# One streaming encoder layer on one core: order of the first loads, stored q weights, and who scales the FFN's sums

## The chip, the core and the metric

The kernel runs on one core of one Trainium2 chip. A core has five engines with a queue of instructions each: TensorE (PE, with PEld for the loads of its weights), VectorE (DVE), ScalarE (ACT), GpSimd (POOL) and SyncE (SP, which here only issues DMAs). Each engine runs its own queue in program order and waits on semaphores for the others. Sixteen DMA engines move the data between the main memory and the core. The metric is the device time of one execution in microseconds. The kernel before took 3031.0 us, the median of three runs (3030.57 to 3031.74).

## The reference

One layer of a streaming encoder over 2048 prompt tokens and 64 sample tokens, in float32, with 1024 channels:

```python
mod = silu(c) @ w_ada + b_ada                  # six vectors of 1024 a token kind
sh1, sc1, gt1, sh2, sc2, gt2 = split(mod, 6)
h = rms_norm(x, norm1_g) * (1 + sc1) + sh1
glu_a, glu_b, q, k, v, g_conv, g_attn = split(h @ w_in, ...)
u = glu_a * sigmoid(glu_b)
conv_out = silu(layer_norm(depthwise_conv(u, 31) + b_dw)) @ w_conv_out
o = attend(rms_norm(q), rms_norm(k), v, rel_bias)      # chunks of 64, a band of 9
merged = sigmoid(g_conv) * conv_out + sigmoid(g_attn) * (o @ w_attn_out)
x = x + gt1 * (merged @ w_o)
h2 = rms_norm(x, norm2_g) * (1 + sc2) + sh2
gate, up = split(h2 @ w_ffn_in)
x = x + gt2 * ((silu(gate) * up) @ w_ffn_out)
```

Beside both streams' x the last rows of the convolution's input and of k and v are given out.

## The kernel before

**Products.** Each float32 factor is split into a high and a low part, and one product is three matmuls (`mm3`). A weight comes as raw floats into a staging buffer (`wst`, `wup` or `wfo`, L370), ACT rounds it to `whi`, and DVE or POOL makes the rest, `wlo<-wst,whi`. The class `Weights` holds five such pairs; `split` (L445) chooses the engine. Weights that several blocks use (`KEPT`, among them the q, k and v columns, key `("qkv", part, k)`) are written to memory as two halves after their first split (L493), and later blocks read both halves.

**Phase 1** goes over blocks of 576, 512, 512 and 512 tokens: norm, q, k and v, the convolution's GLU, gates and attention. Its start (`first_block`, L882) is a piece by itself. The token rows `x_t` are asked for first (L1082, SP), then four 512 KB slabs of `w_ada` (`Slabs.fill`, L241, tile `wmod`, also SP); ACT's queue issues the small vectors (L764 to L769). From `silu(c)`, made of ACT's `th` and written to `cl`, PE makes the slabs' products `pa<-wmod,cl`; DVE copies them to `R`, a product with `sel` turns them, and DVE makes the columns `A` and `B`. The rows of x are scaled by their norm `r` (DVE `t`, POOL `r<-t,mhalf`), turned by PE (`pt<-ident,x_t`), and DVE makes `h<-pt,A,B`, split into `hh` and `hl`. The eight turns of k alternate with modulation's next slabs, and `taps` (L796) loads the convolution's small vectors by SP.

**Phase 2** goes over 576, 768 and 768 tokens (s = 0, 1, 2): merge, `wo`, residual and second norm, FFN. The FFN uses sums of blocks of weights in place of some products; these sums `ws` (two inputs of 128x512) are made by POOL once, at s = 0, and stored in `sum_d` (L417). `presum` (L437) makes the next ones as soon as their raw weights have landed. In `residual` (L1649) a row of tokens gets its mean square (DVE `t`), its `r` by POOL, and ACT scales it to `xn`, which PE turns. PE fills the time with products of the other rows (`wo` over k, of which the first four are shared by all rows of a chunk), and with the first FFN products, `early`.

**The end of a block.** The FFN's sums stand in `acc`, twelve pieces of 128x512 at s = 1 and 2. For these blocks `scale` (L2003) multiplies each piece by the gate row `gt` and then adds the residual input `x1`, both on DVE, one instruction at a time, as a lane of work between the other steps. Then `add_last` (L2029) multiplies the products `pd` of the last two rows of `w_ffn_out` by the gate in PSUM, adds them to `acc`, and sends the piece out (L2045). At s = 0 the gate and x1 are applied at the end by another path.

All arithmetic is issued by one helper (L102), so the profile's groups differ by tile names and shapes. The order of a queue is fixed when the program is built, by lanes of work and an estimate of each engine's load.

Of the kernel before, what the change touches and what calls it, by code (L numbers as in the profile page):

```python
# [229 lines left out]
class Slabs:  # L230


    def __init__(self, sync, pool, stream, keys, source, held):
        self.sync, self.pool, self.stream, self.keys, self.source, self.held = sync, pool, stream, keys, source, held
        self.ready, self.used, self.given, self.freed = [], 0, 0, 0

    def fill(self):
        while len(self.ready) < min(len(self.keys), self.freed + self.held):
            (src,), a, b = self.source(self.keys[len(self.ready)])
            w = self.pool.tile([P, a, b], F32, tag="wmod", name="wmod", bufs=self.held)  # L240
            self.sync.dma_start(w, src)  # L241
            self.ready.append(w)
# [18 lines left out]
class Weights:  # L261
# [5 lines left out]
    def __init__(self, engines, pool, dram, stream, keys, source, staging, held, kept):  # L267
        self.stream = stream
        self.sync, self.act, self.dve, self.gps = engines
        self.pool, self.dram, self.keys, self.source = pool, dram, keys, source  # L270
        self.staging, self.held = staging, held
        self.sum_pool, self.sum_d, self.sums, self.hold, self.landed = None, None, {}, 0, {}

        self.room, self.leaving = {"wst": 1, "wup": 0, "wfo": 0}, {"wst": 0, "wup": 0, "wfo": 0}
# [123 lines left out]
    def operand(self, f, op):  # L398
# [38 lines left out]
    def presum(self):  # L437

        i = len(self.ready)
        if i in self.first and all(self.landed.get(j, 1e18) <= self.stream.load["pe"] for j in self.need[i]):  # L440
            for f, op in self.keys[i][1:]:
                if op[0] == "s":
                    self.operand(f, op)

    def split(self):  # L445
# [17 lines left out]
        on_dve = key[0] in ("in", "qkv") or turn % 2  # L463
# [25 lines left out]
        def then():  # L489
            if key in self.again and key not in self.stored:  # L490
# [21 lines left out]
    def fill(self):  # L512

        while self.available() and len(self.ready) - self.freed < self.held:
            self.split()
# [88 lines left out]
def streaming_layer(ctx: ExitStack, tc: tile.TileContext, I, O):  # L604
# [155 lines left out]
    def setup():  # L760
# [4 lines left out]
        nc.scalar.dma_start(r0[8:16], by_row(I["c_sample"][0]))  # L765
        o = 0
        for name in ("norm1_g", "norm2_g", "b_dw", "conv_ln_g", "conv_ln_b", "b_ada"):
            a = by_row(I[name][0])
            nc.scalar.dma_start(r1[o : o + a.shape[0]], a)  # L769
            o += a.shape[0]  # L770
        pt = ps_g.tile([P, 512], F32, tag="gp", name="pt")
# [4 lines left out]
        act.activation(th, cc, AF.Tanh, scale=0.5)  # L776
        dve.scalar_tensor_tensor(th, th, 1.0, cc, ALU.add, ALU.mult)
        dve.tensor_scalar(cl[:, :, :2], th.rearrange("p (s k) -> p k s", s=2), 0.5, None, ALU.mult)
        dve.memset(cl[:, :, 2:], 0.0)
        dve.memset(sel, 0.0)  # L780
        dve.tensor_reduce(sel[:, :2], ident.rearrange("p (j s) -> p s j", j=4)[:, :2], AX.X, ALU.add)
# [14 lines left out]
        def taps():  # L796
            for i in range(2):
                for j, g in enumerate((I["q_norm_g"], I["k_norm_g"])):
                    nc.sync.dma_start(gqk[HD * i : HD * i + HD, j : j + 1], g.rearrange("o d -> d o"))
            nc.sync.dma_start(gk, I["k_norm_g"].to_broadcast([P, HD]))  # L800
            cc = wk.tile([HIST, CONV], F32, tag="pr", name="cc", bufs=8)
            nc.sync.dma_start(cc, I["cache_conv"][0, 0])
            r2 = wk.tile([TAPS, CONV], F32, tag="pr", name="r2", bufs=8)
            nc.sync.dma_start(r2, I["w_dw"][0])
# [8 lines left out]
        return vectors, taps  # L813
# [64 lines left out]
    def first_rows():  # L878
        places = ((wa, "x", 3), (wa, "x", 3), (wa, "x", 3), (wk, "kk", 1), (wk, "q2", 1))
        return [load_x(*tl, *place) for tl, place in zip(token_tiles(*PBLOCKS[0]), places)]  # L880

    def first_block(xs):  # L882

        tiles = token_tiles(*PBLOCKS[0])
        vectors, taps = setup()
        taps = taps()
        for x_t, (t, n) in zip(xs, tiles):
            r = square(x_t, n)
            dve.tensor_scalar(x_t[:n], x_t[:n], r, None, ALU.mult)

        def modulation(ct):
# [3 lines left out]
            for c6, c in enumerate(cs):  # L895
                mod_sums(pa[:, c], [("mod", c6, ct // 2, h, 0) for h in range(2)])
# [8 lines left out]
        def turn(k):  # L905
# [26 lines left out]
        for k in range(KT - 2):  # L932
            if k == 2:
                next(taps)
# [3 lines left out]
            for i in range(len(tiles)):  # L938
                if i == 2 and not k:
                    rest = modulation(k + 2)  # L940
                if i == (2 if k else 4) and k % 2 == 0:
# [138 lines left out]
    def load_x(t, n, pool, tag, bufs):  # L1080
        x_t = pool.tile([P, D], F32, tag=tag, name="x_t", bufs=bufs)
        nc.sync.dma_start(x_t[:n], rows(x_p, x_s, t, n))  # L1082
# [566 lines left out]
    def residual(pp, t, n, gt1, a, half, hs, free, last, i):  # L1649
# [24 lines left out]
        r = rsqrt_mean(wk, ssq[:n], n, 1, D, 4)  # L1674
        yield stream.when("pool")
# [63 lines left out]
    for s, (lo, hi) in enumerate(CBLOCKS):  # L1739
# [4 lines left out]
        for i, (c0, c1) in enumerate(chunks):  # L1744
# [40 lines left out]
            for k in range(4):  # L1785
                for i in range(len(grp)):
                    wo(i, k)
            for i, (t, n) in enumerate(grp):
                for k in range(4, KT):
# [213 lines left out]
        def scale():  # L2003
# [6 lines left out]
            for i, t, n, j in pieces():  # L2010
                dst = acc[i][:n, 512 * j : 512 * j + 512]
                dve.tensor_tensor(dst, dst, gt[j][:n], ALU.mult)
                yield stream.when("dve")
            yield lambda: "x1" in ends and stream.load["pe"] > ends["landed"]
            for k, (i, t, n, j) in enumerate(pieces()):
                dst = acc[i][:n, 512 * j : 512 * j + 512]
                dve.tensor_tensor(dst, dst, ends["x1"][k // 3][:n, k % 3], ALU.add)
                ends["merged"] = k
                yield stream.when("dve")
# [9 lines left out]
        def add_last(ws):  # L2029

            for k, (i, t, n, j) in enumerate(pieces()):
# [5 lines left out]
                while ends.get("merged", -1) < k:  # L2037
# [5 lines left out]
                stream.at(  # L2043
                    stream.when("dve") + OUT_LAG,
                    lambda t=t, n=n, f=f, dst=dst: nc.sync.dma_start(rows(y_p, y_s, t, n)[:, f], dst),  # L2045
                )
            for _ in ws:
                W.done()

# [87 lines left out]
        stream.flush()  # L2137

# [28 lines left out]
```

## Time and profile before

| what | value |
|---|---|
| median of three runs | 3031.0 us (3030.57 to 3031.74) |
| the profiled execution | 3030.89 us |
| its span | 3029.1 us |
| PE, DVE, ACT, POOL busy | 2936.2, 2123.1, 1286.9, 1071.8 us |
| bytes read from memory, written | 478.63 MB, 148.54 MB |
| mean granted clock of PE | 0.989 |

The span runs from the first to the last instruction that the profile holds; the execution takes 1.8 us more around it. Times in rows are microseconds from the span's start. A row of the timeline has the start, the duration, the engine, the line, the operation, output and inputs, the shapes, how many instructions were merged, and in brackets how long the engine had been idle and what ended that.

### The profile page before, as it was taken

Reading aid. Unit: us, or ns where it says so; the run is one execution under the profiler, and the core shown is the slowest. Engines: PE = TensorE matmul, PEld = TensorE weight load, DVE = VectorE, ACT = ScalarE, POOL = GpSimd, SP = SyncE. Lnnn points to the kernel's source line nnn. Section 1 sums busy time; section 2 is a strip of 40 time slices with the busy share of each in tenths; the row PEclk is TensorE's granted clock in tenths of the full one; section 3 lists DMA queues with packets and bytes.
Section 4 is the critical chain, followed back from the end, with each engine's and each line's share of the span. In section 5 each row is a group of like instructions: output and inputs, shape, how many; then the busy total and the mean of one; then the engine's idle time right before and its main releaser. Section 6 shows DMA issues by size and latency. Waiting matters only on the chain. (4 is left out here: it accounts for less than half of the span.)

```text
span 3029.1 us, 44987 instructions
## 1 busy us (share of the span) xinstructions
PE 2936.2 (97%) x16259; PEld 2603.6 (86%) x16259; DVE 2123.1 (70%) x3884; ACT 1286.9 (42%) x2328; POOL 1071.8 (35%) x681
## 2 busy tenths in 40 slices
PE   7999989999999999989999999999999999999998
PEld 4789867788888788878998899999999899999997
DVE  4888877878877885477677755666667757466668
ACT  2324532452254257464444345534444245344442
POOL 0200210101011102454666443355666341465663
PEclk9999999999999999999999999999999999999999
DMA  9789788888997788885444786333333865333333
GB/s 309 269 300 302 248 288 294 259 271 279 299 288 233 264 255 271 264 286 167 139 149 153 229 265 233 118 97 99 115 119 119 301 218 185 95 97 105 112 119 108
DMA packets 467789, 630.17 MB, mean 208 GB/s; under 512 B 36340, under 2 KB 314728, under 8 KB 467565
## 3 DMA queue, kind: packets, MB, share of 16 engines
q1 hardware_dynamic: 455285, 609.90, 61.9%
q10 hardware_dynamic: 12280, 17.39, 1.6%
q8 instruction: 128, 2.10, 0.3%
q14 instruction: 96, 0.79, 0.1%
HBM read 478.63 MB, written 148.54 MB: 207 GB/s over the span
## 5 line engine op out<-in xcount | busy, mean ns | idle before, releaser
L102 PE MATMUL ps<-t,whi 128*128 128x384 f32 (+1 forms) x2112 | 507.1, 324 | 17.1 <-ACT u L102 8.0
L102 POOL TENSOR_TENSOR wlo<-wst,whi 128x1024 fp32r<-128x1024 f32 (+1 forms) x152 | 349.3, 2308 | 290.7 <-ACT whi L102 237.3
L102 ACT ACTIVATE whi<-wst 128x1024 fp32r<-128x1024 f32 (+1 forms) x261 | 253.5, 975 | 350.2 <-PE ps L102 115.2
L102 PEld LDWEIGHTS ps<-t,whi 128*128 128x128 f32 x2112 | 371.1, 189 | 25.1 <-ACT u L102 11.3
L102 PE MATMUL ps<-b,whi 128*128 128x384 f32 (+1 forms) x1584 | 382.0, 326 | 3.7 <-DVE early L102 2.1
L102 DVE SCALAR_TENSOR_TENSOR y<-u,wd,y 128x512 f32<-128x512 f32 (+1 forms) x480 | 370.2, 772 | 6.0
L102 PE MATMUL ps<-hh,whi 128*128 128x512 f32 (+2 forms) x992 | 362.1, 365 | 0.2 <-DVE part_l L102 0.2
L102 DVE TENSOR_TENSOR acc<-acc,pd 128x512 f32<-128x512 f32 (+1 forms) x464 | 310.6, 685 | 64.7 <-PE pd L102 62.3
L102 PE MATMUL ps<-hh,wlo 128*128 128x512 f32 (+2 forms) x992 | 347.1, 350 | 0.0
L102 PE MATMUL ps<-hl,whi 128*128 128x512 f32 (+2 forms) x992 | 346.3, 349 | 0.0
L102 PE MATMUL ps<-t,wlo 128*128 128x384 f32 (+1 forms) x1056 | 341.2, 323 | 0.7 <-POOL wlo L102 0.7
L102 PE MATMUL pd<-whi,hid 128*128 128x512 f32 (+1 forms) x1016 | 327.8, 393 | 3.9 <-ACT hid L102 3.4
L102 PEld LDWEIGHTS ps<-b,whi 128*128 128x128 f32 x1584 | 279.3, 190 | 9.3 <-DVE early L102 3.0
L102 PE MATMUL ps<-b,wlo 128*128 128x384 f32 (+1 forms) x792 | 257.5, 325 | 0.0
L102 POOL TENSOR_TENSOR r<-t,mhalf 128x1 f32<-128x1 f32 (+3 forms) x68 | 83.5, 1229 | 416.6 <-DVE t L102 400.3
L102 PEld LDWEIGHTS pd<-whi,hid 128*128 128x128 f32 (+1 forms) x1016 | 187.1, 184 | 49.8 <-ACT hid L102 3.9
L102 PEld LDWEIGHTS ps<-hh,wlo 128*128 128x128 f32 x992 | 187.7, 189 | 22.3
L102 PEld LDWEIGHTS ps<-hh,whi 128*128 128x128 f32 x992 | 188.2, 190 | 18.1 <-issue 2.3
L102 PEld LDWEIGHTS ps<-hl,whi 128*128 128x128 f32 x992 | 188.4, 190 | 15.4 <-issue 1.4
L102 PEld LDWEIGHTS ps<-t,wlo 128*128 128x128 f32 x1056 | 199.8, 189 | 1.9 <-POOL wlo L102 1.3
L102 PE MATMUL pd<-wlo,hid 128*128 128x512 f32 (+1 forms) x508 | 199.4, 393 | 0.0
L102 DVE TENSOR_TENSOR wlo<-wst,whi 128x1024 fp32r<-128x1024 f32 (+1 forms) x109 | 136.3, 1256 | 84.3 <-ACT whi L102 80.5
(223 smaller groups left out, 6239.0 us busy)
## 6 DMA issues: line engine op xcount, KB each, us to landing
whi<-w_din_h SPq DMA_DIRECT2D x72, 512.0 KB, 4.7
wlo<-w_din_l SPq DMA_DIRECT2D x72, 512.0 KB, 6.4
wst<-sum_d SPq DMA_DIRECT2D x132, 256.0 KB, 2.8
wfo<-in_w_ffn_out SPq DMA_DIRECT2D x64, 512.0 KB, 4.1
wmod<-in_w_ada SPq DMA_DIRECT2D x48, 512.0 KB, 7.8
sum_d<-ws SPq DMA_DIRECT2D x88, 256.0 KB, 2.2
wst<-in_w_ffn_in SPq DMA_DIRECT2D x84, 256.0 KB, 3.2
wst<-in_w_in SPq DMA_DIRECT2D x36, 512.0 KB, 6.4
```

The lines of the kernel that those rows point to most:

```text
L102: self.last = f(*args, **kw)
```

## The change

It has four parts.

1. The start: the two rows of c, then the first four slabs, by SP's and ACT's queues in turn; then the norm vectors on SP and the x rows on both queues. The first slab sums are ordered ahead of the later rows' scaling and turns; the first weights are split behind them; the first `h` is split in two pieces; `taps` loads by ACT's queue.
2. The q weights (`("qkv", 0, k)`) of block 0 are not stored. Block 1 reads the raw ones again and splits them on ACT and POOL, then stores them.
3. `presum` runs only when weights aren't held back, and sums are placed behind the last residual's `r` on POOL. At s = 0 the last chunk shares six k of `wo` instead of four.
4. `scale` works on POOL. At s = 2 POOL also adds x1; at s = 1 that addition is left to the next block, after `add_last`, and the output follows it.

```diff
 class Slabs:
-            self.sync.dma_start(w, src)
+            i = len(self.ready)
+            (self.other if i < self.held and i % 2 else self.sync).dma_start(w, src)
...
-            elif n == 1 or not kept(key):
+            elif n == 1 or not kept(key) or n == 2 and key[:2] == ("qkv", 0):
...
-            self.gps.tensor_tensor(t, x, y, e)
+            with self.behind():
+                self.gps.tensor_tensor(t, x, y, e)
...
-        if i in self.first and all(...):
+        if not self.hold and i in self.first and all(...):
...
-        on_dve = key[0] in ("in", "qkv") or turn % 2
+        passing = key[:2] == ("qkv", 0) and i < 4
+        on_dve = key[0] == "in" or key[0] == "qkv" and (passing or key[1]) or turn % 2
...
-            if key in self.again and key not in self.stored:
+            if key in self.again and key not in self.stored and not passing:
...
-    def setup():
+    def load_vectors():
         nc.scalar.dma_start(r0[0:8], by_row(I["c_prompt"][0]))
         nc.scalar.dma_start(r0[8:16], by_row(I["c_sample"][0]))
+        yield r0, r1
...
-            nc.scalar.dma_start(r1[o : o + a.shape[0]], a)
+            nc.sync.dma_start(r1[o : o + a.shape[0]], a)
...
+        queues = (nc.sync, nc.sync, nc.scalar, nc.sync, nc.scalar)
...
-            split(hh[:, k], hl[:, k], h)
-        rest = modulation(0)
-        vectors()
-        rest()
-        W.open("wst")
-        turn(0)
+            for c in (slice(0, 448), slice(448, 576)) if not k else (slice(0, 576),):
+                split(hh[:, k, c], hl[:, k, c], h[:, c])
+        with tc.issue_after(begun[0]), tc.issue_after(begun[1]):
+            scale_rows(0, 2)
+            rest = modulation(0)
+            vectors()
+            rest()
+            sums_turned = pe.last.ins
+            with tc.issue_after(dve.last.ins):
+                scale_rows(2, 5)
+            with tc.issue_after(act.last.ins), tc.issue_after(dve.last.ins):
+                W.reach = W.held
+                W.fill()
+        with tc.issue_after(sums_turned):
+            turn(0)
...
-    xs = first_rows()
-    M = Slabs(nc.sync, wa, stream, list(mod_order()), source, 4)
-    M.fill()
+    vectors_ = load_vectors()
+    first_vectors = next(vectors_)
+    M = Slabs(nc.sync, nc.scalar, wa, stream, list(mod_order()), source, 4)
+    M.fill()
+    next(vectors_)
+    xs = first_rows()
...
         r = rsqrt_mean(wk, ssq[:n], n, 1, D, 4)
+        W.behind = lambda ins=gps.last.ins: tc.issue_after(ins)
...
-            for k in range(4):
+            shared = KT - 2 if not s and c1 == hi else 4
+            for k in range(shared):
...
-                dve.tensor_tensor(dst, dst, gt[j][:n], ALU.mult)
+                gps.tensor_tensor(dst, dst, gt[j][:n], ALU.mult)
...
+                if after(k):
+                    continue
+                add_x1(k, i, n, j)
+        def after(k):
+            return s + 1 < len(CBLOCKS)
+        def add_x1(k, i, n, j):
+            dst = acc[i][:n, 512 * j : 512 * j + 512]
+            gps.tensor_tensor(dst, dst, ends["x1"][k // 3][:n, k % 3], ALU.add)
...
+        def add_left(left):
+            for dst, x1, out in left:
+                gps.tensor_tensor(dst, dst, x1, ALU.add)
+                stream.at(stream.when("pool") + OUT_LAG, lambda out=out, dst=dst: nc.sync.dma_start(out, dst))
+                yield stream.when("pool"), {"pool": 500}
...
         work.drain()
         stream.flush()
+        if left:
+            work.add(add_left(left))
```

How the queues stand, at three places. A row here is an instruction or DMA with its shape, and how often it stands there in a row. First ACT's queue at the start of the program, before (`junk,ssq` squares a row of x, `rv` is the relative bias):

```order
L769 DMA r_225<-in_conv_ln_b 4x128
L769 DMA r_225<-in_b_ada 48x128
L102 ACT_TABLE_LOAD
L102 ACTIVATE junk,ssq<-x_t 64x512 x2
L102 ACTIVATE junk,ssq<-x_t 128x512 x2
L102 ACTIVATE th<-cc 128x16
L102 ACTIVATE junk,ssq<-x_t 128x512 x6
L955 DMA rv<-in_rel_bias 8x257
L102 ACTIVATE whi<-wst 128x1024 x3
```

and after:

```order
L773 DMA r_200<-in_c_prompt 8x128
L774 DMA r_200<-in_c_sample 8x128
L244 DMA wmod<-in_w_ada 128x4x256 x2
L1116 DMA x_t<-in_x_prompt 128x1024
L989 DMA rv<-in_rel_bias 8x257
L1116 DMA x_t<-in_x_prompt 128x1024
L102 ACT_TABLE_LOAD
L102 ACTIVATE th<-cc 128x16
L102 ACTIVATE junk,ssq<-x_t 64x512 x2
L102 ACTIVATE junk,ssq<-x_t 128x512 x8
L102 ACTIVATE whi<-wst 128x1024
```

Two slabs, two x rows and the bias have moved onto ACT's queue ahead of `th`, the small vectors have left it, and one split instead of three stands before the first `hh`.

POOL's queue in the middle, where phase 2 begins its first FFN (`r` is a norm, `ws` a sum of weights), before:

```order
L102 TENSOR_TENSOR wlo<-wup,whi 128x1024
L102 TENSOR_TENSOR wlo<-wfo,whi 128x512 x2
L102 TENSOR_TENSOR ws<-wfo 128x512
L102 TENSOR_TENSOR ws<-ws,wup 128x512
L102 TENSOR_TENSOR r<-t,mhalf 128x1
L102 TENSOR_TENSOR wlo<-wst,whi 128x512 x2
L102 TENSOR_TENSOR wlo<-wfo,whi 128x512 x2
L102 TENSOR_TENSOR ws<-wup,wfo 128x512
L102 TENSOR_TENSOR ws<-wup,ws 128x512
L102 TENSOR_TENSOR r<-t,mhalf 128x1
L102 TENSOR_TENSOR ws<-wst 128x512
L102 TENSOR_TENSOR ws<-ws,wst 128x512
```

and after:

```order
L102 TENSOR_TENSOR wlo<-wup,whi 128x1024
L102 TENSOR_TENSOR wlo<-wfo,whi 128x512 x2
L102 TENSOR_TENSOR wlo<-wst,whi 128x512 x2
L102 TENSOR_TENSOR wlo<-wfo,whi 128x512 x2
L102 TENSOR_TENSOR r<-t,mhalf 128x1 x2
L102 TENSOR_TENSOR ws<-wst 128x512
L102 TENSOR_TENSOR ws<-ws,wup 128x512
L102 TENSOR_TENSOR ws<-wup,wst 128x512
L102 TENSOR_TENSOR ws<-wup,ws 128x512
```

Both norms now stand ahead of the four sums that were around them, and behind all four splits.

The end of block s = 1 on DVE, before:

```order
L102 SCALAR_TENSOR_TENSOR ps<-tg,ps 128x384
L102 TENSOR_TENSOR acc<-acc,gt 128x512
L102 TENSOR_TENSOR ps<-ps,v 128x384
L102 TENSOR_TENSOR acc<-acc,gt 128x512 x2
L102 TENSOR_TENSOR hid<-ps,hid 128x384
L102 TENSOR_TENSOR v<-ps,v 128x384
L102 TENSOR_TENSOR acc<-acc,x_23906 128x512 x3
L102 TENSOR_TENSOR ps<-ps,u_23870 128x384
L102 TENSOR_TENSOR acc<-acc,x_23907 128x512 x3
L102 TENSOR_TENSOR ps<-ps,s_23806 128x384
```

and on POOL, after:

```order
L102 TENSOR_TENSOR wlo<-wst,whi 128x1024
L102 TENSOR_TENSOR acc<-acc,gt 128x512 x2
L102 TENSOR_TENSOR wlo<-wfo,whi 128x512
L102 TENSOR_TENSOR acc<-acc,gt 128x512
L102 TENSOR_TENSOR wlo<-wst,whi 128x1024 x2
L102 TENSOR_TENSOR acc<-acc,gt 128x512 x6
L102 TENSOR_TENSOR wlo<-wup,whi 128x1024
L102 TENSOR_TENSOR wlo<-wst,whi 128x512
L102 TENSOR_TENSOR acc<-acc,gt 128x512 x2
L102 TENSOR_TENSOR wlo<-wfo,whi 128x1024
L102 TENSOR_TENSOR acc<-acc,gt 128x512
```

The products by `gt` have gone from DVE's queue and stand between POOL's splits; on DVE the rows with `ps`, `hid` and `v` now follow each other, with only `acc<-acc,pd` between them.

More of the change, by code (lines that the diff above doesn't have):

```diff
@@ L439, in presum @@
         i = len(self.ready)
-        if i in self.first and all(self.landed.get(j, 1e18) <= self.stream.load["pe"] for j in self.need[i]):
+        if not self.hold and i in self.first and all(self.landed.get(j, 1e18) <= self.stream.load["pe"] for j in self.need[i]):
             for f, op in self.keys[i][1:]:
@@ L512, in fill @@
     def fill(self):
-        while self.available() and len(self.ready) - self.freed < self.held:
+        while self.available() and len(self.ready) - self.freed < self.reach:
             self.split()
@@ L879, in first_rows, with scale_rows @@
         places = ((wa, "x", 3), (wa, "x", 3), (wa, "x", 3), (wk, "kk", 1), (wk, "q2", 1))
-        return [load_x(*tl, *place) for tl, place in zip(token_tiles(*PBLOCKS[0]), places)]
+        queues = (nc.sync, nc.sync, nc.scalar, nc.sync, nc.scalar)
+        return [load_x(*tl, *place, q) for tl, place, q in zip(token_tiles(*PBLOCKS[0]), places, queues)]
     def first_block(xs):
         tiles = token_tiles(*PBLOCKS[0])
-        vectors, taps = setup()
+        vectors, taps, begun = setup()
         taps = taps()
-        for x_t, (t, n) in zip(xs, tiles):
-            r = square(x_t, n)
-            dve.tensor_scalar(x_t[:n], x_t[:n], r, None, ALU.mult)
+        def scale_rows(a, b):
+            for x_t, (t, n) in list(zip(xs, tiles))[a:b]:
+                r = square(x_t, n)
+                dve.tensor_scalar(x_t[:n], x_t[:n], r, None, ALU.mult)
         def modulation(ct):
@@ L894, in modulation @@
             cs = [slice(c6 * 2 * P, (c6 + 1) * 2 * P) for c6 in range(2)]
-            for c6, c in enumerate(cs):
-                mod_sums(pa[:, c], [("mod", c6, ct // 2, h, 0) for h in range(2)])
+            with tc.issue_after(pe.last.ins):
+                for c6, c in enumerate(cs):
+                    mod_sums(pa[:, c], [("mod", c6, ct // 2, h, 0) for h in range(2)])
             R = mod_rows(pa)
@@ L933, in first_block @@
             if k == 2:
-                next(taps)
+                with tc.issue_after(act.last.ins):
+                    next(taps)
             turn(k + 1)
@@ L1788, in streaming_layer @@
             for i, (t, n) in enumerate(grp):
-                for k in range(4, KT):
+                for k in range(shared, KT):
                     wo(i, k)
@@ L2036, in add_last @@
                     mm3(ps, h[:, 0, c], h[:, 1, c], w[0][:, 0, f], w[1][:, 0, f], e == last[0], e == last[-1])
-                while ends.get("merged", -1) < k:
+                while ends.get("scaled" if after(k) else "added", -1) < k:
                     work.step(work.gens[0])
@@ L2042, in add_last @@
                 dve.tensor_tensor(dst, dst, ps, ALU.add)
[L2043 to L2046, printed above, removed]
+                out = rows(y_p, y_s, t, n)[:, f]
+                if after(k):
+                    left.append((dst, ends["x1"][k // 3][:n, k % 3], out))
+                else:
+                    stream.at(stream.when("dve") + OUT_LAG, lambda out=out, dst=dst: nc.sync.dma_start(out, dst))
             for _ in ws:
                 W.done()
+        left = []
+        def add_left(left):
[3 more added lines that the diff above has]
+                yield stream.when("pool"), {"pool": 500}
         def add_down(fs, ws):
```

41 lines of the change are left out of this document (24 added, 17 removed).

## The prediction

> **What bounds the kernel now.** I read the page first, then TensorE's waits, then the timeline around each long wait.
>
> ```profile
> span 3029.1 us, 44987 instructions
> PE 2936.2 (97%) x16259; PEld 2603.6 (86%) x16259; DVE 2123.1 (70%) x3884; ACT 1286.9 (42%) x2328; POOL 1071.8 (35%) x681
> ...
> POOL 0200210101011102454666443355666341465663
> ```
>
> TensorE (PE) is busy for 97% of the span, and the change takes no product away. So only PE's idle time, 3029.1 − 2936.2 = 92.9 us, and its time at a lower clock can be won. GpSimd (POOL) is two thirds idle: in the left 16 of 40 slices almost empty, in the others at about half.
>
> ```profile
> PE pt L102 <- DVE h L102: 8.3, 3, 4.1
> PE ps L102 <- ACT u L102: 8.0, 4, 3.7
> ...
> PE ps L102 <- ACT t L102: 6.0, 1, 6.0
> ```
>
> These are PE's waits by releaser: total, times, longest. Three kinds stand out, and the timeline puts them at the start, in the middle and at the ends of the last two blocks of phase 2, which are the places that the diff edits. A long wait costs twice, as PE's windows show (busy, count of matmuls, granted clock, DMA share, GB/s):
>
> ```profile
> 2354.60:2358.60 4.00, 4.00 (x14) 0.50 1.05 389
> 2360.40:2364.40 4.00, 4.00 (x24) 1.00 0.84 290
> 54.80:58.20 3.40, 3.40 (x10) 0.50 0.98 373
> 59.20:62.60 3.40, 3.40 (x20) 1.00 1.09 369
> ```
>
> Just behind a stall the granted clock is 0.50 and 4 us hold 14 matmuls instead of 24. The slow stretch lasts some 5 us, so a stall of 3.5 to 6 us takes about 5 × 10/24 = 2.1 us more; with the slow first product I put 2.5.
>
> **The start.**
>
> ```profile
> 6.33 4.54 SPq L241 DMA_DIRECT2D wmod<-in_w_ada  x4
> ...
> 18.85 1.08 PE L102 MATMUL pa<-wmod,cl 128*32 128x256 f32 x8 [0.39 <-DMA wmod<-in_w_ada]
> ...
> 28.57 0.78 PE L102 MATMUL ps<-whi,hh 128*64 128x512 f32 x1
> ...
> 50.17 1.06 ACT L102 ACTIVATE whi<-wst 128x1024 fp32r<-128x1024 f32 x1 [3.07 <-DMA wst<-in_w_in]
> 51.26 1.23 DVE L102 TENSOR_TENSOR wlo<-wst,whi 128x1024 fp32r<-128x1024 f32 x1 [2.46 <-ACT whi L102]
> ...
> 53.79 1.38 PE L102 MATMUL pt<-ident,x_t 64*128 64x64 f32 x5 [4.02 <-DVE h L102]
> ...
> 28.50:53.00 24.50, 21.09 (x137) 12.54 (x136) 10.61 (x22) 4.04 (x5) 0.00 (x0) 0.98 0.92 299
> ```
>
> Today the four slabs of w_ada are issued behind the x rows, from 6.33 on, and the last of the four slab products ends at 18.85 + 1.08 = 19.93; the first product of q follows 8.6 us later, at 28.57. In the changed program the slabs go first and by two queues, but the activation `th`, from which the products' other operand comes, stands on ScalarE (ACT) behind two x loads. The four issues of 6.33 took 4.54 us for 2 MB; at the 299 GB/s of the last row 2.1 MB are 7 us, so I estimate the slabs landed near 9.5 and, with the x rows behind them at that rate, the ACT queue free for `th` near 13.9. The slab products then run from about 14.4 to 18.4, only 1.5 us earlier than now. Behind them two of three `wlo` splits (1.23 each) leave the path to the first product, and the scaling of three x tiles comes onto it, for which I put 4 to 5. First product: 18.4 + 8.6 − 2.5 + 5 = 29.5 to 30, so **+1.4** (between −2.5, if nothing holds `th`, and +4).
>
> The second stall, 4.02 before 53.79, is a DVE split that waited for its raw weights (50.17 waited 3.07 for the DMA) and stood ahead of `h`. The 16 engines were 0.92 busy then, with the 512 KB writes of the q parts among the reads. The changed program drops eight such writes of block 0 (4.2 MB, 14 us at 299 GB/s), moves the small vectors of `taps` off SyncE's (SP's) queue, and asks for these weights earlier. The stall goes with its slow stretch: −4.0 − 1.8 (less than 2.5, since transposes fill part of it). What is late next there is the next modulation's B and A, without slack worth a number: bounds 0 to −5.8. I add −1 for smaller stalls of the block whose DMA writes are gone. **Start: +1.4 − 5.8 − 1 = −5.4**, between +4 and −10.
>
> The Trainium skill, "DMA: Bandwidth & Descriptors", section "Issuing engines are not separate DMA queues", speaks against expecting much of two queues: it says that DMAs started from different engines share the same 16 engines, and only the time to issue is saved. By it the slabs come no sooner than the bytes allow; the 0.92 agrees.
>
> **The q parts read twice.** At block 1 the raw q weights are read again, half the bytes that the stored halves had, and split once more.
>
> ```profile
> L102 POOL TENSOR_TENSOR wlo<-wst,whi 128x1024 fp32r<-128x1024 f32 x130 | 315.4, 2437 | 282.7 <-ACT whi L102 229.3 <-DMA x_t<-in_x_prompt 11.4 <-DMA wst<-in_w_ffn_in 9.2
> ```
>
> That is 4 × 2.4 us on POOL, in slices where its digits are 0 to 2, so I count 0; if a norm's `r` waits behind a split each time, up to 4 × 1.2 = +5. Nothing excludes a small gain, −2, from the bytes saved.
>
> **The middle: sums behind norms.**
>
> ```profile
> 1325.19 0.15 DVE L102 TENSOR_SCALAR t<-ssq 128x1 f32<-128x1 f32 x1 [0.27 <-ACT xn L102]
> ...
> 1327.16 1.62 POOL L102 TENSOR_TENSOR ws<-ws,wup 128x512 f32<-128x512 f32 x1
> ...
> 1328.74 0.99 POOL L102 TENSOR_TENSOR r<-t,mhalf 128x1 f32<-128x1 f32 x1
> ...
> 1330.97 0.55 PE L102 MATMUL pw<-ident,xn 128*128 128x128 f32 x3 [2.43 <-ACT xn L102]
> ...
> 1332.54 0.15 DVE L102 TENSOR_SCALAR t<-ssq 128x1 f32<-128x1 f32 x1 [1.22 <-ACT xn L102]
> ...
> 1334.65 1.27 POOL L102 TENSOR_TENSOR ws<-wup,wfo 128x512 f32<-128x512 f32 x1
> ...
> 1337.14 0.55 POOL L102 TENSOR_TENSOR r<-t,mhalf 128x1 f32<-128x1 f32 x1
> ...
> 1339.47 0.69 DVE L102 TENSOR_TENSOR wlo<-ws,whi 128x512 fp32r<-128x512 f32 x1 [6.78 <-DMA w_dfi_l<-wlo]
> ...
> 1350.80 0.61 PE L102 MATMUL ps<-t,whi 128*128 128x288 f32 x1 [5.99 <-ACT t L102]
> ```
>
> The norms' `r` were ready to start at 1325.3 and 1332.7 and ran at 1328.74 and 1337.14, behind sums `ws` and splits. In the new order four 128x512 splits (5.0 us) and then both `r` stand ahead of every sum. With the splits' operands of now, POOL gets to the first `r` at about 1331, 2 us later than now, and to the second at 1332.1, 5 us earlier; six `wo` products that wait for no norm fill PE's time before the first. The sums follow from 1332.7, four by 1337.8, and DVE's chain of splits that ends in the 5.99 us wait starts near 1337 instead of 1339.5. I take that wait as 3 us shorter and the first two waits as unchanged in sum: **−3**. If the whole 5.99 and its slow stretch go: −8; if the first `r` costs its 2 us and the sums reach DVE no sooner, +3.
>
> **The ends of the last two blocks.**
>
> ```profile
> 2344.41 1.87 DVE L102 TENSOR_TENSOR acc<-acc,pd 128x512 f32<-128x512 f32 x3
> ...
> 2349.07 2.75 POOL L102 TENSOR_TENSOR wlo<-wfo,whi 128x1024 fp32r<-128x1024 f32 x1 [0.61 <-ACT whi L102]
> ...
> 2350.00 2.37 DVE L102 TENSOR_TENSOR acc<-acc,gt 128x512 f32<-128x512 f32 x1
> ...
> 2353.80 1.01 PE L102 MATMUL ps<-t,whi 128*128 128x384 f32 x2 [3.70 <-ACT u L102]
> ...
> 2363.07 4.09 DVE L102 TENSOR_TENSOR acc<-acc,x 128x512 f32<-128x512 f32 x3
> ...
> 2370.46 0.79 PE L102 MATMUL pd<-whi,hid 128*128 128x512 f32 x1 [3.42 <-ACT hid L102]
> ...
> 2388.38 5.21 POOL L102 TENSOR_TENSOR wlo<-wst,whi 128x1024 fp32r<-128x1024 f32 x2 [16.75 <-ACT whi L102]
> ...
> 2995.19 1.01 PE L102 MATMUL ps<-t,whi 128*128 128x384 f32 x2 [3.70 <-ACT u L102]
> ```
>
> DVE's products by the gate and additions of x1 stand in its queue between the steps that feed the next product. Three accumulations with `pd` took 1.87, about 0.65 each; one product by the gate took 2.37 while POOL's split ran from 2349.07 to 2351.82, and three additions 4.09. Behind the 2.37 comes `ps<-ps,v`, then ACT's `u`, then PE's 3.70; behind the 4.09, PE's 3.42. With both gone from DVE the steps stand as in the blocks' steady part, where PE does not wait. Block s=1: −(3.70 + 2.5 + 3.42 + 2.7) = **−12.3**. Block s=2: −(3.70 + 2.6) = **−6.3**; its additions did not hold PE.
>
> What slowed the 2.37 has a rule: the Trainium skill, "SBUF — State Buffer", section "SBUF: two separate sides", gives a port pair that VectorE with two SBUF inputs and a reading GpSimd instruction take in turns, each for a whole instruction. The 2.37 against 0.65 agrees, as does 1.87 for three that take `pd` from PSUM, beside a POOL split. By it the moved products hold DVE nowhere that matters.
>
> The cost is on POOL. A 128x512 instruction with two inputs took 1.27 (1334.65), so twelve take 15.3 and two sets 30.6 a block; a split behind them is later by what stands ahead of it.
>
> ```profile
> 2332.40 5.30 POOL L102 TENSOR_TENSOR wlo<-wst,whi 128x1024 fp32r<-128x1024 f32 x2 [3.12 <-ACT whi L102]
> ...
> 2344.02 0.34 PE L102 MATMUL ps<-b,wlo 128*128 128x384 f32 x1
> ```
>
> The first split of 2332.40 ends at 2334.8 and is first used at 2344.0, 9.2 us on; by buffer names the others up to 2372 have 10 to 26. In program order at most three products stand ahead of that one (3.8 us), and all twelve before those with more. So POOL keeps up: 0. Block 1's additions of x1 fall mostly into the 16.75 us that POOL idled before 2388.38, and what is late behind them has 10 us. Block 2's start when x1 has landed, near 3000, and run to 3015.4; the last rows need the first at about 3004.7 and the last at 3017.6, 2 us of slack.
>
> The Trainium skill, "GPSIMD Engine Reference", section "4.1 Engine selection", advises the other way: elementwise work on VectorE, GpSimd being about half as fast. 1.27 against 0.65 agrees; it is the second rival's ground.
>
> **Sum**: −5.4 − 3 + 0 − 12.3 − 6.3 = −27.0. The profiled run took 3030.89, the span 3029.1 of it, and the median is 3031.0, so both lead to **3004**.
>
> **Rivals.**
> 1. *POOL is late at the block ends.* If the additions of block 2 start 5 us later than I think, or the waits of POOL's products for `acc` delay splits, the ends give back 12 of 18.6: −27 + 12, 3016. For it: 2 us of slack in block 2. Against it: 9 to 26 us in block 1.
> 2. *Slower.* A product on POOL that waits for DVE's `acc` holds every split queued behind it. If that makes splits late by a set of twelve, 15.3, less the 9.2 of slack, PE stalls 6.1 and runs slow for 2.5 at both ends, in place of the gain there: −8.4 + 17.2 = +8.8, 3040. It decides once a split is over 9 us late. Against it: `acc` is ready before each of its products in DVE's queue now.
> 3. *The slabs do come first.* If `th` does not wait and the chain behind the sums is as long as now, the first product comes 2.5 earlier rather than 1.4 later, and the middle's stall goes whole: −27 − 4 − 5, 2995.
> 4. *The change doesn't do what it says*: `th` behind the x rows and the re-split's cost make the start +4 and +5, POOL gives back 12, and the middle nothing: 4 + 5 − 6.6 = +2.4, 3033.
>
> **Chances**: forecast 0.60; POOL late 0.15; slabs first 0.14; slower 0.04; no effect 0.07. Apart, the terms' bounds run from −10 − 8 − 2 − 18.6 = −38.6 to far above 0; they won't meet all at one end. The range 2991 to 3019 holds the forecast and the cases on either side. About 0.2%, 6 us, can be told from no change: faster (under 3025) 0.89, same 0.07, slower 0.04.
>
> **What would show it.** At the block ends no wait for `u` or `hid` over 1 us and no clock of 0.50; `acc` on POOL at about 1.3 us each; in the middle both `r` ahead of all `ws` and a wait for `t` of about 3; at the start the first product near 30, and no stall of 4 us until q ends. It is wrong if PE waits for `wlo` of POOL, if the last rows wait for POOL's `acc`, or if the first product comes after 33.

## The result, and the profile after

The changed kernel took 3010.26 us, the median of four runs (3003.84 to 3015.84), the kernel before beside it 3031.37 (3030.57 to 3032.77). The ratio is 0.9929, with a 95% interval of 0.9907 to 0.9951: 21.5 us faster, between 15 and 28. The forecast was 3004, and 2991 to 3019 the range. Single executions scatter by some 10 us, and the kernel before does so too where it was run more often (3027.3 to 3040.8 in the batches below), so a difference of a few us is read from intervals, or from where in a profile it arises.

The page of the changed kernel, and TensorE's waits in it (total, times, longest):

```profile
span 3011.3 us, 45036 instructions
PE 2927.7 (97%) x16259; PEld 2599.9 (86%) x16259; DVE 2080.1 (69%) x3836; ACT 1291.3 (43%) x2333; POOL 1136.0 (38%) x734
```

```profile
PE ptp L102 <- DVE pr L102: 10.9, 8, 3.4
...
PE ps L102 <- ACT t L102: 4.6, 1, 4.6
...
PE pt L102 <- DVE h L102: 1.9, 1, 1.9
...
PE ps L102 <- ACT u L102: 1.4, 2, 1.1
```

The same 16259 matmuls are busy for 8.5 us less, at a mean granted clock of 0.990 instead of 0.989, and the idle time is 83.6 us instead of 92.9. The waits for `u`, `hid` and `h` have gone or shrunk. New at the top is `ptp` waiting for `pr`, which is attention.

**Where the time went.** The n-th matmul that TensorE starts can be set beside the n-th of before. The table gives its start in a run less its start in the profile of before, at nine places of the latter's time, so a step between two columns is what a stage gained or lost. At 360, and by a few at 2340, the programs with another order have not run quite the same products as before; at the other places they have. One profile each: a step of 2 or 3 us is no finding.

| us against before, at | 133 | 282 | 360 | 500 | 1320 | 1375 | 2340 | 2420 | last |
|---|---|---|---|---|---|---|---|---|---|
| the change | -10.1 | -13.2 | -3.5 | -4.0 | +0.3 | -1.6 | -0.5 | -10.1 | -17.2 |
| q not read again (e1) | -0.6 | -0.5 | -0.4 | -0.5 | +5.3 | +2.9 | +3.3 | -7.9 | -15.0 |
| only q read again (e2) | -9.7 | -8.9 | -0.1 | -0.7 | -0.1 | +2.1 | +1.2 | -1.5 | -1.7 |
| only the ends (e3) | -0.2 | -1.3 | -0.4 | -1.6 | +3.4 | +5.3 | +5.3 | -5.4 | -12.5 |
| only the start (e4) | +4.1 | +2.7 | +2.7 | +0.1 | +4.8 | +5.3 | +5.1 | +5.1 | +5.1 |
| no q writes (e5) | -7.2 | -8.6 | -6.8 | -9.1 | -5.4 | -5.5 | -4.7 | -5.6 | -5.7 |
| q split again on DVE (e6) | -10.5 | -13.7 | -11.9 | -16.1 | -11.3 | -13.7 | -13.2 | -25.3 | -32.4 |
| x1 by ACT (e7) | -9.2 | -12.9 | -11.3 | -13.0 | -11.1 | -13.4 | -12.4 | -16.5 | -22.1 |
| only the sums (e8) | -1.1 | -2.3 | -1.0 | -2.2 | -1.7 | -4.1 | -3.3 | -5.4 | -6.5 |
| e6 with the old start (e9) | -8.4 | -7.6 | -5.9 | -5.8 | -4.0 | -5.9 | -6.0 | -16.6 | -23.7 |
| e6's order, split on POOL (e10) | -11.6 | -15.4 | -12.6 | -13.6 | -9.5 | -11.9 | -11.5 | -23.2 | -30.3 |
| e6, x1 not left over (e11) | -10.1 | -12.5 | -10.8 | -11.2 | -5.3 | -8.3 | -7.3 | -10.2 | -17.3 |
| only q, split on DVE (e12) | -12.3 | -12.1 | -10.3 | -8.0 | -5.5 | -5.0 | -4.5 | -5.4 | -5.4 |

The first row has the question in it. The change is 13.2 us ahead at 282, nine of which are gone at 500, and the rest by 1320; the ends of the last two blocks then give 17.

**The ends** are as forecast. The first two fences have groups of GpSimd and VectorE between 2328 and 2385 of the changed kernel (the count, then the total in us and the mean of one in ns), the next three have rows of its timeline, and the last one TensorE's window at the end of the last block:

```profile
L102 POOL TENSOR_TENSOR acc<-acc,x 128x512 f32<-128x512 f32 x12 | 15.2, 1290 | 0.2 <-DVE acc L102 0.2
...
L102 POOL TENSOR_TENSOR acc<-acc,gt 128x512 f32<-128x512 f32 x11 | 14.1, 1306 | 0.0
```

```profile
L102 DVE TENSOR_TENSOR acc<-acc,pd 128x512 f32<-128x512 f32 x27 | 17.9, 684 | 0.9 <-PE pd L102 0.7
```

```profile
2364.85 10.07 POOL L102 TENSOR_TENSOR acc<-acc,x 128x512 f32<-128x512 f32 x8 [0.18 <-DVE acc L102]
```

```profile
2368.87 1.28 DVE L102 TENSOR_TENSOR acc<-acc,pd 128x512 f32<-128x512 f32 x2
...
2371.30 1.28 DVE L102 TENSOR_TENSOR acc<-acc,pd 128x512 f32<-128x512 f32 x2
```

```profile
2378.71 0.44 PE L102 MATMUL ps<-cin,whi 128*128 128x384 f32 x1 [1.60 <-DMA cin<-o_d]
```

```profile
2975.00:3000.00 25.00, 25.00 (x130) 1.00 0.49 174
```

An instruction on GpSimd takes 1.29 or 1.31. VectorE's accumulations from PSUM take 0.64 each in the ten us in which GpSimd adds x1 without a pause, as before (0.62), and TensorE waits nowhere between 2340 and 2377, nor between 2975 and 3000. What is late next is the following block's input: 1.60 for `cin`.

**The middle.** Two of TensorE's waits in the kernel before, beside the 2.43 and 5.99 of the prediction:

```profile
1338.92 0.55 PE L102 MATMUL pw<-ident,xn 128*128 128x128 f32 x3 [0.55 <-ACT xn L102]
1340.59 0.54 PE L102 MATMUL ps<-b,whi 128*128 128x288 f32 x2 [1.12 <-DVE early L102]
```

GpSimd, VectorE and TensorE in the changed kernel:

```profile
1331.29 0.55 POOL L102 TENSOR_TENSOR r<-t,mhalf 128x1 f32<-128x1 f32 x1
1332.02 0.55 POOL L102 TENSOR_TENSOR r<-t,mhalf 128x1 f32<-128x1 f32 x1 [0.18 <-DVE t L102]
1332.54 1.29 POOL L102 TENSOR_TENSOR ws<-wst 128x512 f32<-128x512 f32 x1
```

```profile
1337.12 1.08 DVE L102 TENSOR_TENSOR wlo<-ws,whi 128x512 fp32r<-128x512 f32 x1 [5.18 <-ACT whi L102]
```

```profile
1329.60 0.53 PE L102 MATMUL ps<-b,whi 128*128 128x288 f32 x2 [0.72 <-ACT early L102]
...
1338.94 0.53 PE L102 MATMUL ps<-b,whi 128*128 128x288 f32 x2 [2.40 <-DVE early L102]
...
1342.25 0.81 PE L102 MATMUL ps<-b,whi 128*128 128x288 f32 x2 [0.29 <-ACT early L102]
...
1348.96 0.61 PE L102 MATMUL ps<-t,whi 128*128 128x288 f32 x1 [4.57 <-ACT t L102]
```

Norms, sums and DVE's chain stand within half a us of where the prediction put them (1331, 1332.1, 1332.7, 1337). The waits that were 2.43, 0.55, 1.12 and 5.99 are 0.72, 2.40, 0.29 and 4.57.

**The start**, TensorE in the changed kernel:

```profile
13.35 3.64 PE L102 MATMUL pa<-wmod,cl 128*32 128x256 f32 x32 [1.32 <-DVE cl L102]
...
28.84 0.78 PE L102 MATMUL ps<-whi,hh 128*64 128x512 f32 x1
...
47.59 0.71 PE L102 MATMUL pa<-sel,R 128*128 128x128 f32 x4 [1.70 <-DVE R L102]
```

All slab products run in one row, held by `cl` (that is, by `th`) and not by a slab; the first product of q comes 0.3 later than before, and the longest wait from there to the end of q is 1.70 instead of 4.02.

### The profile page after: what moved, and what is told of

It is laid out like the page before. It is cut to its first block, busy times and chain, and to the rows that moved or that the text cites. A ratio compares the mean times of both kernels' runs of the same rounds, so it can differ in the third digit from the quotient of the medians.

```text
span 3011.3 us, 45036 instructions
## 1 busy us (share of the span) xinstructions
PE 2927.7 (97%) x16259; PEld 2599.9 (86%) x16259; DVE 2080.1 (69%) x3836; ACT 1291.3 (43%) x2333; POOL 1136.0 (38%) x734
## 4 chain that ended last, share of the span: by engine, by line
PE 79%; DVE 9%; DMA 6%; ACT 2%; issue 2%; POOL 2%; SPq 0%; ACTq 0%; POOLq 0%; DVEq 0%
PE ps L102 49%; PE pd L102 15%; PE pw L102 6%; DVE y L102 3%; PE po L102 2%; PE sc L102 2%; PE ptp L102 2%; DVE wlo L102 1%; PE pa L102 1%; PE pt L102 1%; DVE pr L102 1%; DMA wst<-in_w_in 1%; ACT whi L102 1%; POOL r L102 1%; POOL wlo L102 1%
## 5 line engine op out<-in xcount | busy, mean ns | idle before, releaser
L102 POOL TENSOR_TENSOR wlo<-wst,whi 128x1024 fp32r<-128x1024 f32 (+1 forms) x157 | 357.9, 2290 | 272.2 <-ACT whi L102 258.2
L102 PEld LDWEIGHTS ps<-b,whi 128*128 128x128 f32 x1584 | 278.8, 190 | 12.1 <-DVE early L102 4.2
```

The costliest lines, as they stand in the source:

```text
L102: self.last = f(*args, **kw)
```

## The experiments

Each is the kernel before or after with the edit shown. Where an edit undoes or keeps a whole part of the change, its lines stand above under the change. A time is a median, with the ratio to the kernel before of the same batch and the 95% interval.

### Is it the second reading of q? (e1, e2, e3, e4)

The four parts were taken apart. e1 undoes the second part in the changed kernel, e2, e3 and e4 are the second, fourth and first part alone.

The diff is e1's:

```diff
-            elif n == 1 or not kept(key) or n == 2 and key[:2] == ("qkv", 0):
+            elif n == 1 or not kept(key):
...
-        on_dve = key[0] == "in" or key[0] == "qkv" and (passing or key[1]) or turn % 2
+        on_dve = key[0] in ("in", "qkv") or turn % 2
...
-            if key in self.again and key not in self.stored and not passing:
+            if key in self.again and key not in self.stored:
```

> The change without its second part: the q halves are written at block 0 and read at block 1, as before. Theory A (the second reading of q at block 1 makes the program put the attention heads of block 0 where no products stand beside them, and this gives back the start's gain between 315 and 361): the gain of the start stays until 360, about -9 there instead of -3.5, and the whole is near 3001 (2997 to 3005). Rival B (a later stage of block 1 is bound by something else and takes back whatever the start gained): -3.5 at 360 again, and the whole near 3010. Rival C (the start's gain itself comes from the writes that are left out): -5 or less already at 282, and the whole near 3012.

3012.83 us (0.9934, 0.9919 to 0.9949). With q written at block 0 as before, the gain at 133 is 0.6 and there is nothing to give back: rival C for the start, against A. The whole can't be told from the change's.

> Only the second part: q halves not written at block 0, raw q read and split again at block 1. Theory A: some gain at the start (0 to -6) and +9 between 325 and 365, so 3031 to 3040. Rival B: no difference behind 365, 3031. Rival C: -6 to -9 at 282 and kept, 3022 to 3025.

3032.54 us (1.0000, 0.9991 to 1.0009). The second part alone wins 9.7 us up to 133 and loses 8.8 between 282 and 360. That fits A or B, and not C, by which the gain is kept.

> Only the fourth part: products by the gate and additions of x1 on GpSimd. If the ends of the blocks gain by themselves what the whole change shows there (-12.6 with 2.7 given back at the next block's first loads, and -7): 3031 - 17 = 3014 (3012 to 3016), in a narrow spread. Rival (part of it comes with the other parts' order): 3018 or more.

3014.86 us (0.9943, 0.9928 to 0.9958), 17.4 us: the ends by themselves. Their two steps in the table, -10.7 and -7.1, return in every kernel that has them, leaves x1 over and loads it by SP (-9.6 to -12.1, and -7.1). The first step is made of two: up to the matmul that stood at 2376 of before, all eight programs with the fourth part gain 12.6, and what they give back comes behind it, at the next block's inputs.

> Only the first part: slabs first by two queues, later rows' scaling behind the sums, vectors on other queues; the q writes stay. Theory A: -5 at 81, -8 to -13 at 282, kept: 3018 to 3024. Rival B: given back behind 300, 3028 to 3031. Rival C: -2 at 81 and 3029.

3034.24 us (1.0007, 0.9997 to 1.0016): nothing. All three theories were wrong here in what they expected at 81 and 282: while the q halves are still written, the new start is 4 us ahead at 60, and 3.5 us behind at 81.

So the gain at 282 comes with the writes left out: the nine programs without them are 7.6 to 15.4 us ahead there, the four with them between 2.3 ahead and 2.7 behind. What follows block 0 takes nine back in the change. Whether any early gain would be taken back (B), or only one that is bought with the second reading (A), was still open.

### Gain without the second reading (e5)

e5 leaves the eight writes of q out of the kernel before, and blocks 1 to 3 multiply by k's weights in q's place, so their q is left out of the result:

```diff
-            for t, d in zip((hi, lo), self.stored[key][0]):
+            other = ("qkv", 1, key[2]) if key[:2] == ("qkv", 0) else key
+            for t, d in zip((hi, lo), self.stored[other][0]):
...
+            if key[:2] == ("qkv", 0):
+                self.stored[key] = None, shape
             if key in self.again and key not in self.stored:
```

> The kernel before without the eight writes of the q halves; blocks 1 to 3 read the k halves in their place, so the bytes read, the splits and the program's order are those of before, and q is left out of those blocks' result. Theory A (the writes cost about 9 us up to 133; what gives it back at 320 to 360 is the second reading's order of the attention heads on TensorE): about -9 at 282 and still at 360, the whole near 3023 (3019 to 3027). Rival B (block 1 is bound by something that takes back whatever came before): -9 at 282, 0 at 360, the whole near 3032.

3024.58 us (0.9976, 0.9967 to 0.9985). Of 8.6 us at 282, 6.8 are there at 360 and 5.7 at the end. Block 1 does not take back what was won before it: B falls. One thing in the expectation does not hold: TensorE's order is not that of before between 27 and 82, where products of `w_ada`'s slabs stand earlier (it is e2's order). Whether the bytes or this order win the 7 us is not separated.

### The second split on the other engine (e6, e12, e10)

What does the second reading do at 320? These are TensorE's rows in the changed kernel, and its windows there (busy, matmuls, granted clock, DMA share, GB/s), first of before, then of the change:

```profile
320.53 0.41 PE L102 MATMUL sc<-kk,q 128*128 128x128 f32 x2 [0.67 <-DMA kk<-k_d]
322.19 0.71 PE L102 MATMUL sc<-kk,q 128*128 128x256 f32 x2 [1.25 <-DVE sm L102]
323.42 1.01 PE L102 MATMUL sc<-kk,q 128*128 128x384 f32 x2 [0.53 <-DVE sm L102]
324.23 0.41 PE L102 MATMUL ptp<-ident,pr 128*128 128x128 f32 x1
325.09 1.22 PE L102 MATMUL sc<-kk,q 128*128 128x512 f32 x2 [0.45 <-DVE sm L102]
326.11 0.63 PE L102 MATMUL ptp<-ident,pr 128*128 128x128 f32 x2
327.63 0.90 PE L102 MATMUL ptp<-ident,pr 128*128 128x128 f32 x3 [0.90 <-DVE pr L102]
```

```profile
325.00:345.00 20.00, 18.01 (x117) 1.00 0.80 253
```

```profile
312.00:332.00 20.00, 16.22 (x85) 0.76 0.75 233
```

A head of block 0's attention stands in TensorE's queue with none of the large products between its steps, so after the first, which waits for `kk`, most of them wait for the softmax (`sm`, `pr`), and the granted clock of the window is 0.76. The order is made when the program is built, from an estimate of each engine's load; four splits billed to GpSimd move it. Billed to VectorE, they move it otherwise, and products stand between the head's steps:

```diff
-        on_dve = key[0] == "in" or key[0] == "qkv" and (passing or key[1]) or turn % 2
+        on_dve = key[0] in ("in", "qkv") or turn % 2
```

> The whole change, with the second split of q on VectorE as the first, not on GpSimd. In this program no attention head stands without products beside it where block 0 ends. Theory A: about -12 at 282 and at least -9 at 360, the whole near 3002 (2997 to 3006). Rival B: -4 at 360 and 3010. Rival D (the raw weights' loads and ACT's four roundings are what costs, not the order): -4 to -6 at 360, 3008.

3001.28 us (0.9899, 0.9876 to 0.9921), the lowest median of all, though the interval overlaps the change's. Of 13.7 us at 282, 11.9 are there at 360. In the same stretch its window, and the longest wait of the head, read:

```profile
311.00:331.00 20.00, 17.92 (x126) 1.00 0.88 284
```

```profile
329.85 0.44 PE L102 MATMUL ptp<-ident,pr 128*128 128x128 f32 x2 [1.39 <-DVE sm L102]
```

The second part alone with this line, on the kernel before:

> The kernel before with the second part alone, q split again on VectorE. Theory A: the 9 us of the start are kept behind 360, the whole near 3023 (3019 to 3027), as where the writes were only left out. Rival: the second reading costs what the writes saved, 3031.

3026.13 us (0.9979, 0.9970 to 0.9988), against 1.0000 (0.9991 to 1.0009) for e2: the one line is worth about 6 us, and the intervals are apart. The raw loads and ACT's roundings are in both, so they are not the cost. Left were GpSimd's time and the order. e10 bills the splits to VectorE and runs them on GpSimd; TensorE's order is that of e6 but for four places, where a single step stands some rows earlier or later:

```diff
+            if key[:2] == ("qkv", 0) and not passing:
+                args = lo[:, c], src, hi[:, c].bitcast(F32), ALU.subtract
+                self.stream.add("dve", "tensor_tensor", 1024, args, {})
+                self.gps.engine.tensor_tensor(*args)
+            else:
+                e.tensor_tensor(lo[:, c], src, hi[:, c].bitcast(F32), ALU.subtract)
```

> The version that splits q again on VectorE in the planner's books, so that TensorE's order at block 1 is that version's, but the four splits run on GpSimd, as in the change. Theory A (the order of the attention heads is what gave the start's gain back): the gain at 360 stays, -11 or more, the whole near 3002 (2997 to 3006). Rival E (GpSimd's 2.4 us splits ahead of the norms' r are what costs): -4 at 360, 3010.

In its profile 12.6 of 15.4 us are kept at 360 (window below), as theory A has it, and the profiled execution took 3000.25. The median is 3006.12 (0.9918, 0.9902 to 0.9935), between the two expectations, and its interval overlaps both e6's and the change's. The stretch is settled by the profiles: from 282 to 360 all six programs with this order lose 1.6 to 2.9 us, and the two with the change's order 9.7 and 8.8. That GpSimd's splits cost a few us elsewhere is not excluded.

```profile
309.00:329.00 20.00, 17.34 (x125) 1.00 0.85 272
```

### Is the new start worth anything with the writes gone? (e9)

The version e6 with the start of before (first part undone).

> The version that splits q again on VectorE, with the start of before: x rows first, one queue for the slabs, vectors by ACT. If the new start adds to the writes left out (13.7 us won at 282 with it, 8.6 without): about 5 us slower than the version with it, near 3006 (3003 to 3009). Rival (the start's order is worth nothing here either, as it was alone): 3001.

3003.03 us (0.9908, 0.9893 to 0.9923) against 0.9899 (0.9876 to 0.9921): no difference that can be told. The 6 us between the two profiles at 282 are little more than profiles differ by: e12, whose program is the same as e9's up to there, has 12.1. All five profiles with the new start and no q writes have 12.5 to 15.4 at 282, and all four with the old one 7.6 to 12.1, so some 4 us may be won there, which the times do not show.

### The sums alone (e8)

> Only the third part: sums of weights behind the norms, six shared k of wo. If it does by itself what the whole change shows between 1320 and 1375: about -2 to -4 there against programs of the old order, the whole 3029 (3027 to 3031). Rival (nothing): 3032.

3028.09 us (0.9988, 0.9979 to 0.9997), 3.6 us, the step from 1320 to 1375 being -2.4. Six of the seven other programs with the new order have -1.9 to -2.4 there and one -3.0; five with the old order have -0.1 to +2.2.

### The addition left to the next block (e11, e7)

In e11 GpSimd adds x1 at s = 1 before the last products, as at s = 2 (base: e6):

```diff
         def after(k):
-            return s + 1 < len(CBLOCKS)
+            return False
```

> The version that splits q again on VectorE, and at s = 1 GpSimd adds x1 before the last products, as at s = 2, instead of in the next block. If GpSimd then becomes the bound at that end (my rival of a late GpSimd: twelve more instructions of 1.3 us between its splits): a wait of TensorE for DVE's acc of 2 to 8 us before 2370, the whole 3 to 10 above 3001. If GpSimd has room: 3001.

3011.10 us (0.9929, 0.9908 to 0.9950), 9 above e6. The step from 2340 to 2420 is -3.0 instead of -12.1. TensorE's waits there:

```profile
2360.60 0.50 PE L102 MATMUL pd<-whi,hid 128*128 128x512 f32 x1 [0.81 <-DVE acc L102]
2369.18 0.50 PE L102 MATMUL pd<-whi,hid 128*128 128x512 f32 x1 [1.05 <-DVE acc L102]
...
2391.96 0.98 PE L102 MATMUL ps<-cin,whi 128*128 128x384 f32 x2 [3.70 <-DVE t L102]
```

Up to the matmul at 2376 of before e11 has gained 12.6, as the others. Behind it the two waits for VectorE's `acc`, which itself waits for GpSimd, cost some 3 us: the forecast's rival of a late GpSimd, in small. The larger part, some 6 us, comes at the third wait, which a DMA ended. These are VectorE's row ahead of that wait, and SP's queue:

```profile
2391.26 0.55 DVE L102 SCALAR_TENSOR_TENSOR t<-tg,ps 128x384 f32<-128x384 f32 x1 [7.16 <-DMA tg<-g_d]
```

```profile
2376.73 9.41 SPq L2099 DMA_DIRECT2D out<-acc  x12
2386.22 2.28 SPq L1103 DMA_DIRECT2D tg<-g_d  x4
```

With nothing left over, the twelve output pieces are issued together, ahead of the next block's gates `tg`; in e6 the outputs go out a few at a time behind and between the `tg` loads. So leaving the addition over pays more by the order of the DMAs than by GpSimd's time. No run moves the outputs alone, and the intervals of e11 and e6 overlap, so this is read from the profiles.

In e7 the loads of x1 at s = 1 go to ACT's queue, to free SP for `cin`, and GpSimd's additions start later (base: e6; the lines that call the loads):

```diff
+        if s and s + 1 < len(CBLOCKS):
+            load_x1(nc.scalar)
         if s:
             add_last(ws)
```

> As the run before, and the twelve loads of x1 at s = 1 are issued by ACT's queue behind its last hid, not by SP ahead of the next block's weights and inputs. If the 1.6 and 1.0 us waits of TensorE at 2377 and 2391 come from SP's 11 us of x1 issues ahead of the loads of cin and tg: both are gone, and the step from 2340 to 2420 is about -12.5 instead of -9.6, the whole 2.5 to 3 below the run before. Rival (GpSimd's additions, now later, hold the splits behind them): a wait for wlo near 2390 to 2400 and no gain.

3012.55 us (0.9933, 0.9918 to 0.9948), 11 slower than e6 by the medians, with intervals that just touch, for a reason that its expectation had not named. ACT's queue, and TensorE's next wait:

```profile
2356.26 19.55 ACTq L2082 DMA_DIRECT2D x<-x_d  x12
2375.93 2.95 ACT L102 ACTIVATE whi<-wst 128x1024 fp32r<-128x1024 f32 x3 [25.46 <-DMA x<-x_d]
```

```profile
2379.90 1.01 PE L102 MATMUL ps<-cin,whi 128*128 128x384 f32 x2 [6.49 <-DVE m L102]
```

Twelve issues held ACT for 19.55 us, and the roundings and the `m` queued behind them came only after that. The step from 2340 to 2420 is -4.1 instead of -12.1. Whether SP's x1 issues cause the 1.60 wait for `cin` stays open: e6 has the same SP order, and no such wait of over 0.5 us in its profile.

## Why the prediction was right, and where not

- **The ends** (-18.6 forecast): right in mechanism and size. The part alone measured -17.4, its steps -10.7 and -7.1 against -12.3 and -6.3. Up to 2376 the first was 12.6, and some of it (1.9 us in e3's profile) comes back at the next block's first inputs, which the sum had left out. POOL at no cost was right as the change stands; in e11 it cost some 3 us.
- **The middle** (-3): -1.9 in the change's profile step, -2.4 in e8's, -3.6 in e8's time. The 5.99 wait shrank by 1.4, not by 3, and the waits ahead of it, taken as unchanged, by 0.7.
- **The start** (-5.4): at 81, where q ends, the change is 5.3 ahead, and by 282, 13.2. That the number fits at 81 is luck, since its parts are others. "Drops eight such writes" carries it: leaving them out alone is 6.5 ahead at 81 and wins 7.5 in time, while the new start alone is 3.5 behind at 81. In time the rest of the new order is worth nothing that can be told, alone (1.0007) or with the writes gone (e9). The term for the first product was +1.4 (the sum as written, 29.5 against 28.57, gives +0.9) and measured +0.3: the slab products ended 1.4 earlier than forecast, at 16.99, and the chain behind them took 11.9 us.
- **"The q parts read twice … so I count 0"** is the step that failed. It looked for the cost on POOL, in slices where its digits are 0 to 2, and POOL had the room. It cost 9 us on TensorE between 282 and 500: the same four splits entered the planner's loads, and the order came out with an attention head alone. e10 keeps the engine and not the order, and the stretch keeps its gain. The changed order stood in TensorE's queue, at a place that the prediction did not look at, since the diff moves nothing there by its words.
- Forecast terms and measurement: -5.4 + 0 became about 0 (e2 and e4 show no gain alone, the change -4.0 at 500 and nothing at 1320), -3 became -3.6, -18.6 became -17.4. That the total came within 6 us of the forecast owes something to luck: a gain of 13.2 at 282 in place of 5.4, and a cost of 9 in place of 0, nearly cancel. Parts alone sum to -18.8 from their ratios, and the change measured -21.5 with 15 to 28.
- Rival 3 (slabs first) did not come: the slab products waited for `cl`, not for a slab. Rival 1 (POOL late) did not come in the change, where TensorE waits for POOL's `acc` nowhere at the ends; that 3010 lies between the forecast and this rival's 3016 has the cause above.

The loss between 360 and 1320 of the changed kernel, 3.8 us, was not traced. Four of the other programs lose 4 to 6 there, four others less than 1; of the rest none loses over 3.1.

## What to carry to other kernels

Where an order is planned from estimated loads, a change that moves work to an idle engine can cost time in a place that it doesn't touch: compare the whole order on the engine that bounds, and look for steps that have lost the work beside them. Moving elementwise work off a busy engine pays when it stood between the steps of a chain, even at twice the duration, provided that what the last steps wait for is left until later. Look at the DMA queue too: outputs that are issued together can stand ahead of the next stage's loads, as in e11. Where a write is issued matters: with the q halves written one block later (e12, 0.9979) the kernel was as fast as with none written (e5, 0.9976); why they cost more at the start is not shown.

## What the runs showed of the hardware

Issuing DMAs can hold a queue for long: twelve 256 KB loads took ACT's queue 19.55 us at the end of a block (e7), and SP's 10.90 in the changed kernel, where single issues near by took 0.3 to 0.5. What held them is not shown; the DMA engines' busy share was 1.04 and 1.00 in these stretches.

```profile
2353.21 10.90 SPq L2078 DMA_DIRECT2D x<-x_d  x12
```

On ACT, which also computes, the roundings behind the loads waited for all of it.
